# Encoder block on one core: f32 products and turns of an attention item side by side, queries normed inside the softmax, weight remainders and LN0 rows on VectorE

## The chip, the cores and the metric

The kernel runs on one core of a Trainium2 chip. Its time is device time in microseconds (us), from the start of the program on the core to its end; the times of the kernel before are those of three runs. The engines are named as the profile names them: PE is TensorE's matrix multiply (PEld its weight loads), DVE is VectorE, ACT is ScalarE, POOL is GpSimd, SP the engine that issues the DMAs.

## The reference, cut to what matters

One encoder layer for 512 tokens of width 1024, in float32: LayerNorm, a mixer of two attention branches, LayerNorm, an expert layer with 16 experts, LayerNorm.

```python
h = layer_norm(x, ln0_g, ln0_b)
proj = h @ w_in                                   # 1024 -> 5120, split into the parts below
qa, ka, va, qb, kb, vb, ga, gb = split(proj)      # 512, 128, 128, 768, 768, 768, 1024, 1024
# branch A: 8 query heads, 2 key heads, 64 wide
qa = rms_norm(qa, qn_g);  ka = rms_norm(ka, kn_g) # over the 64 of a head: y * rsqrt(mean(y*y) + eps) * gain
qa = rotary(qa, row, column); ka = rotary(ka, row, column)
ya = softmax(qa @ ka.T / 8) @ va @ w_branch_a
# branch B: 12 heads, three windows (128, 512, 2048) with strides 1, 4 and 16
qb = partial_rotary(qb); kb = partial_rotary(kb)
yb = combine(dilated_attention(qb, kb, vb)) @ w_branch_b
mix = (sigmoid(ga + b) * ya + sigmoid(gb + b) * yb) @ w_out
h = layer_norm(alpha * h + mix)
h = layer_norm(alpha * h + expert_choice_swiglu(h))   # each expert takes 64 tokens
```

## The kernel before

**Precision.** A matrix product of the mixer is three passes of the type fp32r: a value is split into a high part (`A.copy` into an fp32r tile) and the remainder (value minus high part), and `mm3` (lines 241 to 244) multiplies high by high, low by high and high by low. A call of `mm3` on 128x512 is a *unit*. Products of the attention on probabilities and the turns (transposes by a product with the identity) are plain f32.

**Weights.** `w_in` and the branch weights come in 46 tiles of 128x1024. `split(i)` (L211) lets ACT write the high part and POOL the remainder (L221); `split_to` keeps the splits two to three tiles ahead of the units that use them. A tile is used by eight units.

**Order.** The schedule is written by hand. Chunk 0 (the queries of branch A) is multiplied first. The other chunks of `w_in` stand as units in a queue (`gemm_units`, L402), with other work hooked in behind the n-th unit of a chunk: the norm and rotary of chunk 0 (`chain0a` to `chain0d`, and the turns `t_q`) run inside the units of chunk 1, those of keys in chunk 2 (`chain1a`, `chain1b`, `t_k`), the rotary of branch B (`rope_b` by `chain2`, `chain_b`) and its turns (`t_k0`, `t_b`) in chunks 3 to 5. `fill(ns)` takes units off the queue for so many ns, 650 each.

**Branch A** (from L756) has 16 items (a pair of heads and a block of 128 queries). Step n of its loop turns the probabilities of item n-1 (`a_trans`, two heads), computes the scores of item n (`a_scores`, fp32r), their softmax (`a_soft`: DVE finds the maximum, ACT takes exp, `a_norm`: DVE divides by the sum), and multiplies the turned probabilities of item n-1 with the values (`a_pv`). Six units are spread over it in four places. **Branch B** (from L842) does the same with 8 items and seven units in four places; its scores are f32.

[...]

**After the mixer** come the output product, LN1, the router with a top-64 search on DVE (TensorE multiplies idle products meanwhile, `keep_clock`), and 16 experts, whose 403 MB of weights stream through a ring of buffers; a buffer is loaded again when an expert has used it. The ring's first loads start as the mixer's buffers come free.

Of the kernel before, what the change touches and what calls it, by code (L numbers as in the profile page):

```python
# [47 lines left out]
def encoder_block(ctx, tc, x, ln0_g, ln0_b, w_in, b_gate, qn_g, kn_g, w_branch_a, w_branch_b,  # L48
# [53 lines left out]
    bPT = [misc[:, u0 + (4 + i) * 512:u0 + (5 + i) * 512] for i in range(2)]  # L102
# [107 lines left out]
    def split(i):  # L210
# [166 lines left out]

    def fill_until(name):
# [16 lines left out]
    def gemm_units(c, perm, evac, later=()):  # L395
# [4 lines left out]
        for kk in range(4):  # L400
            for m in range(NT):
                for j in range(2):  # L402
# [18 lines left out]
                    if k == KT - 1:  # L421
                        queue.append((0.0, lambda m=m: evac(m)))
# [56 lines left out]
    def chain0d(m):
        q4 = qhl[m % 2].rearrange("p (h v d) -> p h v d", h=8, v=2)  # L480
        t = heads(atmp[2 + m % 2])
        V.tensor_tensor(t, t, heads(atmp[m % 2]), OP.add)
        A.copy(q4[:, :, 0, :], t)
        V.tensor_tensor(q4[:, :, 1, :], t, q4[:, :, 0, :].bitcast(F32), OP.subtract)
# [41 lines left out]
    def chain1b():  # L526
        x4 = xall[:, :, 0:128].rearrange("p i (h d) -> p i h d", h=2)
        V.tensor_tensor(x4, x4, ssk.unsqueeze(3).to_broadcast([P, NT, 2, 64]), OP.mult)
        G.tensor_tensor(kt[0].rearrange("p i (h d) -> p i h d", h=2), x4,
                        ra[:, :, 128:192].unsqueeze(2).to_broadcast([P, NT, 2, 64]), OP.mult)  # L530
        for h in range(2):
            x5 = xall[:, :, h * 64:(h + 1) * 64].rearrange("p i (a b d) -> p i a b d", a=2, b=2)
            t5 = kt[1][:, :, h * 64:(h + 1) * 64].rearrange("p i (a b d) -> p i a b d", a=2, b=2)
            s5 = ra[:, :, 192:256].rearrange("p i (a b d) -> p i a b d", a=2, b=2)
            for b in range(2):
                V.tensor_tensor(t5[:, :, :, b, :], x5[:, :, :, 1 - b, :], s5[:, :, :, b, :], OP.mult)
# [91 lines left out]
    for m in range(NT):  # L628
        evac(0)(m)
# [1028 lines left out]
```

## Time and profile before

| | us |
|---|---|
| median of three runs (lowest to highest) | 1401.22 (1400.83 to 1401.72) |
| the profiled execution: device time | 1400.32 |
| its span, first to last instruction | 1398.2 |
| busy: PE, DVE, ACT, POOL | 1293.7, 431.3, 267.1, 155.2 |
[...]
| read from HBM, over the span | 437 MB, 314 GB/s |

Busy time is a sum over the span; where the span goes is read from the waits of PE stage by stage and from the chain of work that ended last. Matmuls overlap in the profile: one of 128x512 is shown as 0.39 to 0.40 us and the next starts 0.23 us after it, so the distance of two starts is its cost.

### The profile page before, as it was taken

The page shows a single profiled execution, that of the slowest core. Times are in us where ns is not written, and L with a number is a line of the kernel's source. Part 1 is how long each engine was busy: PE and PEld are TensorE (multiplying, and loading weights), DVE is VectorE, ACT ScalarE, POOL GpSimd, SP SyncE. Part 2 cuts the span into 40 slices and gives each one's busy share as a digit, 9 for nine tenths or more (in the row PEclk, how much of TensorE's full clock was granted, in tenths as well). Part 3 has the DMA queues.
Part 4 walks back from the last instruction along what each step waited for, and adds up shares of the span by engine and source line. Part 5 has one row for each costly group of instructions (what it writes and reads, how often), then busy time and mean ns, then how long its engine had stood idle before and what let it go on. Part 6 is the DMA issues. An engine that isn't in the chain of part 4 may idle for free.

```text
span 1398.2 us, 15300 instructions
## 1 busy us (share of the span) xinstructions
PE 1293.7 (93%) x6393; PEld 656.8 (47%) x6393; DVE 431.3 (31%) x805; ACT 267.1 (19%) x561; POOL 155.2 (11%) x75
## 2 busy tenths in 40 slices
PE   7899899999999899999999889879979988997994
PEld 6688798777787334333333223323322332332343
DVE  7755664556465213030021011102002011210206
ACT  4343344553234010010000000100001000010101
POOL 2544242224420000000000000000000000000001
PEclk9999999999999999999999999999999999999997
DMA  7111111114468789999999999999999999999995
GB/s 262 56 60 46 46 47 59 46 61 149 126 246 337 289 364 429 427 428 427 427 427 427 429 427 427 428 427 427 428 428 428 427 428 427 427 428 427 428 376 182
DMA packets 61323, 440.05 MB, mean 315 GB/s; under 512 B 7659, under 2 KB 23323, under 8 KB 36935
## 3 DMA queue, kind: packets, MB, share of 16 engines
q1 hardware_dynamic: 61255, 439.08, 76.6%
q8 instruction: 50, 0.82, 0.2%
q14 instruction: 18, 0.15, 0.0%
HBM read 436.96 MB, written 2.10 MB: 314 GB/s over the span
## 4 chain that ended last, share of the span: by engine, by line
PE 66%; DMA 25%; DVE 7%; ACT 1%; issue 0%; SPq 0%; DVEq 0%; ACTq 0%
DMA ring<-in_w_up_e_dram 20%; PE ps_o L1427 14%; PE ps_pj L1390 14%; PE ps_pj L242 7%; PE ps_pj L243 6%; PE ps_pj L244 6%; DMA ring<-in_w_down_e_dram 4%; PE ps_x L1440 4%; PE ps_x L1338 4%; PE ps_o L744 1%; PE ps_x L730 1%; PE ps_pj L1492 1%; PE ps_x L1354 1%; PE ps_x L1410 1%; DVE misc L476 1%; PE ps_x L821 0%
## 5 line engine op out<-in xcount | busy, mean ns | idle before, releaser
L1390 PE MATMUL ps_pj<-ring,misc 128*64 128x512 f32 x2032 | 449.9, 595 | 55.2 <-DMA ring<-in_w_up_e_dram 30.1
L1390 PEld LDWEIGHTS ps_pj<-ring,misc 128*64 128x64 f32 x2032 | 144.5, 137 | 351.4 <-issue 294.1
L1427 PE MATMUL ps_o<-ring,misc 128*64 128x512 f32 x928 | 218.5, 602 | 4.2 <-DVE misc L440 2.1
L1403 DVE SCALAR_TENSOR_TENSOR misc<-misc,gate,ps_pj 128x512 f32<-128x512 f32 x32 | 23.8, 747 | 445.8 <-PE ps_pj L1390 367.3
L1427 PEld LDWEIGHTS ps_o<-ring,misc 128*64 128x64 f32 x928 | 58.8, 136 | 136.1 <-issue 124.0
L221 POOL TENSOR_TENSOR whl<-misc,whl 128x1024 fp32r<-128x1024 f32 x38 | 92.6, 2443 | 210.0 <-ACT whl L216 189.6
L1551 POOL TENSOR_TENSOR merged<-merged,misc 128x512 f32<-128x512 f32 x2 | 3.0, 1486 | 939.3 <-ACT merged L1548 939.3
L242 PE MATMUL ps_pj<-whl,hT 128*128 128x512 f32 x192 | 90.5, 471 | 0.2 <-ACT hT L333 0.2
L1402 ACT ACTIVATE misc<-ps_pj 128x512 f32<-128x512 f32 x32 | 19.0, 597 | 364.9 <-PE ps_pj L1390 364.9
L243 PE MATMUL ps_pj<-whl,hT 128*128 128x512 f32 x192 | 78.5, 409 | 1.7 <-DVE hT L336 1.7
L244 PE MATMUL ps_pj<-whl,hT 128*128 128x512 f32 x192 | 78.0, 406 | 0.0
L1442 DVE TENSOR_TENSOR merged<-merged,ps_x 128x512 f32<-128x512 f32 x56 | 38.5, 687 | 102.9 <-PE ps_x L1440 102.9
L1359 ACT ACTIVATE misc<-ps_x,ln_bcol,ln_gcol 128x64 f32<-128x64 f32 x64 | 25.8, 403 | 210.1 <-DVE misc L1361 210.1
L1440 PE MATMUL ps_x<-misc,cst 128*128 128x512 f32 x112 | 63.0, 645 | 0.0
L1338 PE MATMUL ps_x<-hbuf,misc 128*64 128x512 f32 x256 | 59.5, 608 | 1.2 <-DVE misc L1325 1.2
L242 PE MATMUL ps_pj<-hT,whl 128*128 128x512 f32 x128 | 53.5, 418 | 0.9 <-DVE misc L688 0.9
L1361 DVE TENSOR_SCALAR misc<-ps_x,ln_gcol,ln_bcol 128x64 f32<-128x64 f32 x64 | 22.0, 344 | 104.5 <-PE ps_x L1354 81.8
L243 PEld LDWEIGHTS ps_pj<-whl,hT 128*128 128x128 f32 x192 | 50.2, 261 | 6.1 <-DVE hT L336 2.4
L242 PEld LDWEIGHTS ps_pj<-whl,hT 128*128 128x128 f32 x192 | 48.8, 254 | 7.3 <-issue 2.1
L244 PEld LDWEIGHTS ps_pj<-whl,hT 128*128 128x128 f32 x192 | 49.0, 255 | 4.5
L244 PE MATMUL ps_pj<-hT,whl 128*128 128x512 f32 x128 | 50.1, 392 | 0.0
L243 PE MATMUL ps_pj<-hT,whl 128*128 128x512 f32 x128 | 50.0, 391 | 0.0
(320 smaller groups left out, 1359.0 us busy)
## 6 DMA issues: line engine op xcount, KB each, us to landing
ring<-in_w_gate_e_dram SPq DMA_DIRECT2D x63, 2048.0 KB, 30.6
ring<-in_w_up_e_dram SPq DMA_DIRECT2D x62, 2048.0 KB, 27.0
ring<-in_w_down_e_dram SPq DMA_DIRECT2D x57, 2048.0 KB, 31.2
misc<-in_w_in_dram SPq DMA_DIRECT2D x22, 512.0 KB, 3.6
ring<-in_w_down_e_dram SPq DMA_DIRECT2D x12, 512.0 KB, 8.5
misc<-in_w_in_dram SPq DMA_DIRECT2D x20, 256.0 KB, 3.0
misc<-in_w_out_dram SPq DMA_DIRECT2D x8, 512.0 KB, 4.6
b_qk<-in_w_in_dram SPq DMA_DIRECT2D x6, 512.0 KB, 7.0
```

The lines of the kernel that those rows point to most:

```text
L221: G.tensor_tensor(lo, r, hi.bitcast(F32), OP.subtract)
L242: T.matmul(out_, sh, mh, start=start, stop=False)
L243: T.matmul(out_, sl, mh, start=False, stop=False)
L244: T.matmul(out_, sh, ml, start=False, stop=stop)
L1338: T.matmul(pg[64 * g:64 * g + 64, :], oneh[:, m, s * CAP:(s + 1) * CAP], zk[:, :, 4 * g:4 * g + 4], start=m == 0, stop=m == NT - 1)
L1359: A.activation(xeT[e % 2][:, k, :], src, AF.Identity, bias=bcol[:, k:k + 1], scale=gcol[:, k:k + 1])
L1361: V.tensor_scalar(xeT[e % 2][:, k, :], src, gcol[:, k:k + 1], bcol[:, k:k + 1], op0=OP.mult, op1=OP.add)
L1390: T.matmul(gu[which][t // 2][(t % 2) * 64:(t % 2) * 64 + 64, :], xe[:, k, :], w[:, kk % 2, :, 4 * t:4 * t + 4], start=k == 0, stop=k == KT ...
L1403: V.scalar_tensor_tensor(hh[t], sg[t], gate[e], gu[1][t], op0=OP.mult, op1=OP.mult)
L1427: T.matmul(py[n * 64:n * 64 + 64, :], hTe[:, j, :], w[:, n * 512:(n + 1) * 512], start=i == 0, stop=i == 15)
L1440: T.matmul(po, scat[:, m, :], ye[:, n * 512:(n + 1) * 512], start=True, stop=True)
L1442: V.tensor_tensor(a, a, po, OP.add)
```

## The change

- **Order on PE.** In branch A the two turns of item n-1, one turn for branch B (held back in the list `side` by `turn` and given out one per item, or all at once by `flush`) and the probability product of item n-2 stand in one group, straight in front of the scores; then come three units, the division, three units. In branch B the turns, the product of item n-2 and the scores stand together, then seven units. `bPT` gets two more buffers in `gb`.
- **Queries.** The queries aren't normed before the scores. The squares are summed aside, and the factor goes into the exp's scale and the maximum's factor (`qsc`). The rotary works on whole rows: ACT writes a copy with halves swapped (`q_copies`), DVE multiplies twice and adds (`q_turn`). The keys are multiplied by their factor after the rotary, and their swap is on ACT too.
- **POOL's work to DVE.** From tile 4 on the weight remainder is DVE's, and the LN0 gain and bias (two operations of 128x1024 per block on POOL) become 16 of 128x512 on DVE, two in each of the first 8 items.
- **Evictions.** In branch A's loop 7 of 8 evictions by `copy_any` go to ACT, in place of every second one, and branch A's turns are evicted by it too. The first three evictions of chunk 0 and the table product `ra` move ahead.
- **Router.** `keep_clock` runs 36 products in place of 30 during the search and 5 more ahead of the gather.

```diff
-    bPT = [misc[:, u0 + (4 + i) * 512:u0 + (5 + i) * 512] for i in range(2)]
+    bPT = [misc[...] for i in range(2)] + [gb[:, (1 + i) * 512:(2 + i) * 512] for i in range(2)]
...
-            G.tensor_tensor(lo, r, hi.bitcast(F32), OP.subtract)
+            (G if i < 4 else V).tensor_tensor(lo, r, hi.bitcast(F32), OP.subtract)
...
-    def ln0_gain(i):
-        G.tensor_tensor(hbuf[:, i, :], hbuf[:, i, :], gb[:, 0:1024], OP.mult)
-        G.tensor_tensor(hbuf[:, i, :], hbuf[:, i, :], gb[:, 1024:2048], OP.add)
+    def ln0_gain(n):
+        c = slice(n % 2 * 512, n % 2 * 512 + 512)
+        t = hbuf[:, n // 2, c]
+        V.tensor_tensor(t, t, gb[:, 0:1024][:, c], OP.mult)
+        V.tensor_tensor(t, t, gb[:, 1024:2048][:, c], OP.add)
...
+    def turn(fn):
+        return lambda: fn() if side[0] is None else side[0].append(fn)
+    def flush():
+        while side[0]:
+            side[0].pop(0)()
...
+    def q_copies(m):
+        A.copy(atmp[m].rearrange("p (h b d) -> p h b d", b=2, d=16), swapped(xtmp[m]))
+        A.activation(sq[m], xtmp[m], AF.Square)
+    def q_turn(m):
+        V.tensor_tensor(heads(xtmp[m]), heads(xtmp[m]), ra[:, m, 0:64]..., OP.mult)
+        V.tensor_tensor(heads(atmp[m]), heads(atmp[m]), ra[:, m, 64:128]..., OP.mult)
+        V.tensor_tensor(xtmp[m], xtmp[m], atmp[m], OP.add)
+    def q_split(m):
+        A.copy(q4[:, :, 0, :], t)
+        V.tensor_tensor(q4[:, :, 1, :], t, q4[:, :, 0, :].bitcast(F32), OP.subtract)
+    def q_sums(m):
+        V.tensor_reduce(ssq[:, m, :], heads(sq[m]), axis=AX.X, op=OP.add)
+    def q_scale():
+        rms_scale(ss)
+        rsqrt(ss, NT * 8, "q")
+        for v in range(2):
+            V.tensor_scalar(qsc[:, v], ssq, (SCALE, -SCALE)[v], None, op0=OP.mult)
...
     gemm_units(1, False, evac(1), [
-        (2, lambda: (chain0a(2), chain0a(3), chain0b())), (3, lambda: (chain0c(0), chain0c(1), chain0d(0))),
-        (8, ...), (12, ...), (16, lambda: t_q(0)), (17, ...), (20, lambda: t_q(1)), (21, ...), (26, lambda: t_q(2)), (30, lambda: t_q(3))])
+        (1, lambda: (q_copies(1), q_split(0), q_turn(1))), (3, lambda: (q_copies(2), q_split(1), q_turn(2))),
+        (7, lambda: q_copies(3)), (9, lambda: t_q(0)), (10, lambda: (q_split(2), q_turn(3))), (14, lambda: t_q(1)),
+        (15, lambda: (q_split(3), q_sums(0), q_sums(1))), (17, lambda: (q_sums(2), q_sums(3), q_scale())),
+        (21, lambda: t_q(2)), (24, lambda: t_q(3))])
...
     for n in range(len(items) + 1):
         if n >= 1:
-            a_trans(prev, 0)
-            fill(UNIT)
-            a_trans(prev, 1)
-            fill(UNIT)
+            for s in range(2):
+                a_trans((n - 1) % 2, s)
+            if side[0]:
+                side[0].pop(0)()
+        if n >= 2:
+            a_pv(*items[n - 2], n % 2)
         if n < len(items):
             st = a_scores(*items[n])
-            sm = a_soft(st, n % 2)
+            sm = a_soft(*items[n], st, n % 2)
...
-        fill(2 * UNIT)
+        if n < 8:
+            ln0_gain(n)
+        fill(3 * UNIT)
         if n < len(items):
             a_norm(sm, n % 2)
-        if n >= 1:
-            a_pv(*items[n - 1], prev)
-        fill(2 * UNIT)
+            fill(3 * UNIT)
...
-    keep_clock(30)
+    keep_clock(36)
...
+    keep_clock(5)
```

**PE in branch A**, from the turns of one item on. Before (L730 the turns, L242 to L244 a unit, L707 and L708 the scores; the product L744 follows two units later):

```order
L730 MATMUL ps_x<-cst,merged 128x128 x4
L242 MATMUL ps_pj<-whl_70,hT_67 128x512
L243 MATMUL ps_pj<-whl_70,hT_68 128x512
L244 MATMUL ps_pj<-whl_70,hT_67 128x512
L730 MATMUL ps_x<-cst,merged 128x128 x4
L242 MATMUL ps_pj<-whl_70,hT_67 128x512
L243 MATMUL ps_pj<-whl_70,hT_68 128x512
L244 MATMUL ps_pj<-whl_70,hT_67 128x512
L707 MATMUL ps_x<-a_qk 128x512
L708 MATMUL ps_x<-a_qk 128x512
```

Now, in the same place (L748 the turns, L581 a turn for branch B, L759 the product of the item before, L724 and L725 the scores):

```order
L748 MATMUL ps_x<-cst,merged 128x128 x8
L581 MATMUL ps_x<-cst,misc 128x128 x2
L759 MATMUL ps_o<-merged,misc 64x128 x8
L724 MATMUL ps_x<-a_qk 128x512
L725 MATMUL ps_x<-a_qk 128x512
L724 MATMUL ps_x<-a_qk 128x512
L725 MATMUL ps_x<-a_qk 128x512
L242 MATMUL ps_pj<-whl_69,hT_67 128x512
L243 MATMUL ps_pj<-whl_69,hT_68 128x512
L244 MATMUL ps_pj<-whl_69,hT_67 128x512
```

The units that stood between the f32 groups now stand behind the scores, and f32 and fp32r change places once per item.

**DVE in the twelfth item** (n = 11), where chunk 5 begins. Before (L715 and L716 the maximum, L722 and L725 the division, L500 to L504 the rotary):

```order
L715 TENSOR_REDUCE asm<-ps_x 128x1
L716 TENSOR_SCALAR asm<-asm 128x1
L715 TENSOR_REDUCE asm<-ps_x 128x1
L716 TENSOR_SCALAR asm<-asm 128x1
L722 RECIPROCAL asm<-asm 128x2
L725 TENSOR_SCALAR merged<-merged,asm 128x512 x2
L500 TENSOR_TENSOR misc<-misc,cst 128x512
L502 TENSOR_TENSOR misc<-misc,cst 128x32x8 x2
L504 TENSOR_TENSOR misc<-misc 128x32x16
```

Now (L732 and L734 the maximum, L221 the weight remainder, L517 to L521 the rotary, L740 and L743 the division):

```order
L732 TENSOR_REDUCE asm<-ps_x 128x1
L734 TENSOR_SCALAR asm<-asm,qsc 128x1
L732 TENSOR_REDUCE asm<-ps_x 128x1
L734 TENSOR_SCALAR asm<-asm,qsc 128x1
L221 TENSOR_TENSOR whl_70<-misc,whl_70 128x1024
L517 TENSOR_TENSOR misc<-misc,cst 128x512
L519 TENSOR_TENSOR misc<-misc,cst 128x32x8 x2
L521 TENSOR_TENSOR misc<-misc 128x32x16
L740 RECIPROCAL asm<-asm 128x2
L743 TENSOR_SCALAR merged<-merged,asm 128x512 x2
```

A remainder and a rotary have come in between the maximum and the division.

**ACT in chunk 1**, around the query norm. Before (L460 the squares, L143 and L144 the root, L483 the high part of the queries, L438 a turn's eviction):

```order
L460 ACTIVATE misc<-misc 128x512 x4
L143 ACTIVATE q_y<-ssq 128x32
L144 ACTIVATE q_y<-q_y 128x32
L483 CAST a_qk<-misc 128x8x64 x2
L216 CAST whl_70<-b_qk 128x1024
L438 CAST a_qk<-ps_x 128x4x128
```

Now (L452 a turn's eviction, L490 the high part of the queries):

```order
L452 CAST a_qk<-ps_x 128x4x128
L490 CAST a_qk<-misc 128x8x64
L216 CAST whl_69<-b_qk 128x1024
L143 ACTIVATE q_y<-ssq 128x32
L144 ACTIVATE q_y<-q_y 128x32
L452 CAST a_qk<-ps_x 128x4x128 x2
```

The root stood ahead of all turns and now stands between the evictions of the second turn and of the third and fourth.

## Rows read from the trace of the kernel before

**Rows 1.** Windows: PE, PEld, DVE, ACT, POOL busy (count), PE clock, DMA share, GB/s.

```profile
41.00:75.40 34.40, 28.29 (x130) 22.93 (x129) 27.87 (x35) 12.29 (x22) 18.40 (x9) 0.90 0.11 31
...
100.50:237.00 136.50, 130.10 (x774) 116.12 (x774) 78.87 (x158) 54.03 (x111) 48.58 (x20) 0.96 0.16 47
```

**Rows 2.** The chain that ended last, in the expert stage: start us, us, what.

```profile
674.65 26.15 DMA ring<-in_w_up_e_dram
```

**Rows 3.** Waits of PE, 28 to 465 us: total us, times, longest.

```profile
PE ps_x L491 <- DVE a_qk L484: 6.1, 2, 3.3
PE ps_x L730 <- DVE merged L725: 4.7, 1, 4.7
PE ps_o L744 <- DVE merged L734: 1.6, 1, 1.6
...
PE ps_pj L242 <- DVE misc L688: 0.9, 1, 0.9
```

**Rows 4.** Windows behind the third wait and around the L688 wait (columns of Rows 1).

```profile
110.00:113.00 3.00, 3.00 (x11) 2.35 (x10) 1.07 (x4) 0.83 (x3) 0.07 (x1) 0.50 0.00 0
...
371.00:376.00 5.00, 4.06 (x18) 3.05 (x17) 2.36 (x3) 1.95 (x2) 2.91 (x2) 1.00 0.46 164
```

**Rows 5.** Timeline, DVE and POOL in chunk 1: start us, us, engine, line, operation.

```profile
63.56 2.54 POOL L221 TENSOR_TENSOR whl<-b_qk,whl 128x1024 fp32r<-128x1024 f32 x1
...
64.41 2.25 DVE L482 TENSOR_TENSOR misc<-misc 128x512 f32<-128x512 f32 x1
```

**Rows 6.** Timeline, one item of branch A: scores, softmax, DVE and ACT between.

```profile
201.72 0.40 PE L242 MATMUL ps_pj<-whl,hT 128*128 128x512 f32 x1
...
202.15 0.68 DVE L715 TENSOR_REDUCE asm<-ps_x 128x1 f32<-128x512 f32 x1
...
202.43 0.40 PE L242 MATMUL ps_pj<-whl,hT 128*128 128x512 f32 x1
...
204.85 0.88 DVE L725 TENSOR_SCALAR merged<-merged,asm 128x512 f32<-128x512 f32 x2
...
204.98 1.07 ACT L216 CAST whl<-misc 128x1024 fp32r<-128x1024 f32 x1
```

**Rows 7.** Timeline, the same item: PE behind the product, then two groups of turns.

```profile
204.70 0.40 PE L243 MATMUL ps_pj<-whl,hT 128*128 128x512 f32 x1
...
205.87 0.60 PE L730 MATMUL ps_x<-cst,merged 128*128 128x128 f32 x4
...
206.31 0.60 PE L572 MATMUL ps_x<-cst,misc 128*128 128x128 f32 x4
...
207.10 0.40 PE L243 MATMUL ps_pj<-whl,hT 128*128 128x512 f32 x1
```

**Rows 8.** Timeline: single operations of DVE and ACT with nothing beside them on POOL.

```profile
196.22 0.57 ACT L438 COPY misc<-ps_pj 128x512 f32<-128x512 f32 x1
...
197.35 0.68 DVE L500 TENSOR_TENSOR misc<-misc,cst 128x512 f32<-128x512 f32 x1
...
388.33 1.23 DVE L934 TENSOR_TENSOR whl<-merged,whl 128x1024 fp32r<-128x1024 f32 x1 [6.78 <-ACT whl L933]
```

**Rows 9.** Timeline, DVE in the item in which chunk 4 begins.

```profile
150.04 5.08 DVE L502 TENSOR_TENSOR misc<-misc,cst 128x256 f32<-128x256 f32 x2
...
155.77 0.16 DVE L722 RECIPROCAL asm<-asm 128x2 f32<-128x2 f32 x1
```

**Rows 10.** Timeline, branch B: scores, the last sum of exp, a later table load.

```profile
270.12 1.71 PE L792 MATMUL ps_x<-b_qk 64*128 64x128 f32 x16
...
276.04 0.19 ACT L815 ACTIVATION_READ_ACCUMULATOR misc<-misc,bng 128x1 f32 x1
...
283.42 1.28 ACT L815 ACT_TABLE_LOAD   x1 [1.14 <-DVE bng L813]
```

**Rows 11.** The chain (start us, us, what): the router's gather and a later one.

```profile
460.79 5.38 PE ps_x L1338 x16
...
596.62 3.43 PE ps_x L1338 x16
```

More of the change, by code (lines that the diff above doesn't have):

```diff
@@ L101, in encoder_block @@
     bP = [misc[:, u0 + i * 512:u0 + (i + 1) * 512] for i in range(4)]
-    bPT = [misc[:, u0 + (4 + i) * 512:u0 + (5 + i) * 512] for i in range(2)]
+    bPT = [misc[:, u0 + (4 + i) * 512:u0 + (5 + i) * 512] for i in range(2)] + [gb[:, (1 + i) * 512:(2 + i) * 512] for i in range(2)]
     atmp = [misc[:, 4096 + i * 512:4096 + (i + 1) * 512] for i in range(4)]
@@ L421, in gemm_units @@
                     if k == KT - 1:
+                        if m == 0:
+                            queue.append((0.0, flush))
                         queue.append((0.0, lambda m=m: evac(m)))
@@ L526, in chain1b, with half @@
     def chain1b():
[L527 to L536, printed above, removed]
+        x3 = xall[:, :, 0:128]
+        def half(t, b):
+            return t.rearrange("p i (h b d) -> p i h b d", b=2, d=16)[:, :, :, b, :]
+        for b in range(2):
+            A.copy(half(kt[1], b), half(x3, 1 - b))
+        for t, src, c in ((kt[0], x3, 128), (kt[1], kt[1], 192)):
+            for h in range(2):
+                hs = slice(64 * h, 64 * h + 64)
+                V.tensor_tensor(t[:, :, hs], src[:, :, hs], ra[:, :, c:c + 64], OP.mult)
         V.tensor_tensor(kt[1], kt[1], kt[0], OP.add)
+        k4 = kt[1].rearrange("p i (h d) -> p i h d", h=2)
+        V.tensor_tensor(k4, k4, ssk.unsqueeze(3).to_broadcast([P, NT, 2, 64]), OP.mult)
         t = kt[1].rearrange("p i (h d) -> p i h d", h=2)
@@ L649, in gate_bias @@
         V.tensor_copy(bg, pt[:, 0:16])
-    gemm_units(5, True, evac5, sorted(after(chain_b, lambda m: t_b(2, m)) + [(24, gate_bias)], key=lambda t: t[0]))
+    gemm_units(5, True, evac5, after(chain_b, lambda m: t_b(2, m)) + [(24, gate_bias)])
     def evac_gate(c):
@@ L730, in a_trans @@
             T.transpose(pt[:, kt * P:(kt + 1) * P], aP[2 * par + s][:, kt * P:(kt + 1) * P], ident)
[L731 to L734 removed]
+        copy_any(aPT[2 * par + s], pt)
     ob = {}
@@ L843, in encoder_block @@
     items += [(g, p, 0) for g in (1, 2) for p in range(2)]
-    for n in range(len(items) + 1):
-        if n >= 1:
-            b_trans(n - 1, 0)
-            fill(2 * UNIT)
-            b_trans(n - 1, 1)
-            fill(1 * UNIT)
+    for n in range(len(items) + 2):
         if n < len(items):
             fill_until("chain2" if items[n][0] == 0 else "chunk5")
+            flush()
+        if 1 <= n <= len(items):
+            for s in range(2):
+                b_trans(n - 1, s)
+        if n >= 2:
+            g, p, ii = items[n - 2]
+            b_pv(g, p, ii, n - 2, g > 0 or ii == 1)
+        if n < len(items):
             st = b_scores(*items[n])
             b_soft(*items[n], st, n)
-        fill(2 * UNIT)
-        if n >= 1:
-            g, p, ii = items[n - 1]
-            b_pv(g, p, ii, n - 1, g > 0 or ii == 1)
-        fill(2 * UNIT)
+        fill((7 if n < len(items) else 1) * UNIT)
+    side[0] = None
     def nat(ap, g):
```

79 lines of the change are left out of this document (32 added, 47 removed).

## Prediction

> **What bounds the kernel now.** I read the windows by stage first, then the chain of waits, then PE's own waits, then the timeline of the stages that the change touches. In the expert stage PE waits for weights: one step of the chain is a wait of 26.15 us for a ring load [rows 2]. But that stream starts when the mixer's buffers come free and runs on from the first expert's use of them, so whatever the mixer and the router save or lose moves the end by the same amount. Up to there PE is the bound; what can be won is its waits, its clock and its own work. The waits between 28 and 465 us are few: 6.1 us for two query turns, 4.7 and 1.6 us in branch A, 0.9 us later [rows 3]. All have DVE as releaser. [...] Chunk 1 has a mean clock of 0.90 over 34.4 us: 0.10 x 34.4 = 3.4 us lost [rows 1], some 1.7 us behind each of its waits. Branch A has 0.96 over 136.5 us: 5.5 us, of which PE was idle in part; I count 3.9.
>
> **The change part by part.** The sum is made against the profiled execution, 1400.3 us, 0.9 under the median.
>
> *Queries in chunk 1.* Before, the turns wait for the norm, which stands first. Now the norm isn't in their way. From the end of chunk 0 (41 us) DVE does, ahead of the first turn, an eviction, three operations of a rotary, a remainder and a query remainder: 5 x 0.68 + 1.23 = 4.6 us [rows 8], while PE has nine units of 0.71, the distance of two in rows 6: 6.4 us. So the first two waits, 6.1 us, and their 3.4 us of clock go: -9.5. What comes late next: the second half of the fourth turn needs the PSUM buffer of the third turn's first half (three buffers go round), whose eviction now stands on ACT behind the root of the queries, and that waits for DVE's sums. DVE's work up to there: 4 rotaries of 3, 4 query remainders, an eviction, 2 turn copies, 4 sums, all at 0.68, and 3 remainders at 1.23: 23 x 0.68 + 3.7 = 19.3, with 1.5 us of waiting for ACT's high parts 20.8; then the copy, 0.57, behind two small operations of ACT, some 0.5: 62.9 us. PE is there after 24 units and three and a half turns of 8 x 0.11 [rows 7]: 41 + 17.0 + 3.1 = 61.1. A wait of 1.8 (0 to 3, as ACT's part is rough), with 1.7 us of clock behind it, as behind the 1.6 us one. Chunk 1: -9.5 + 3.5 = -6.0, between -9.5 and -3.
>
> *Groups on PE.* From rows 7: eight turns and one product take 207.10 - 205.87 = 1.23 us, where 8 x 0.11 (four turns take 0.44) and 0.235 would do: each passage through f32 costs 0.12. From 202.43 [rows 6] to 204.70 lie four fp32r products and the sixteen of L744: 2.27 less 0.94 and 8 x 0.11 leaves 0.45 for that group. Two of three passages of an item go; a product into half of the columns may keep its own price between turns and scores. So 2 x 0.12 per item at least, 0.12 + 0.45 at most: 16 items give 3.8 to 9; I take 4.5, near the lower end, since the column change stays. Branch B, 8 items, two of four passages: 2 to 5, I take 2.5.
>
> *DVE in branch A* is where the change can lose. DVE's slack: the first maximum starts at 202.15, the first half of the division ends 3.14 us later [rows 6]; the first head's scores are done two products (0.47) before the scores end, so DVE can start some 0.26 before that end. So the turns are ready 2.95 us behind the scores, PE comes after six units of 0.71 = 4.23: 1.3 us to spare. Into the queue between maximum and division come: (a) LN0, two operations, 1.4 us in 8 items; exp takes most of that time, so 0.6, hidden. (b) In 4 of 16 items (n = 3, 7, 11, 15) a remainder. It waits for its high part, which ACT writes after both exps (1.07), then takes 1.23: 2.4 us late, 1.1 us of wait, three times. (c) n = 11: an eviction on ACT (0.57) and a rotary (2 x 0.68 + 2 x 0.42 = 2.2) as well: 4.0. (d) n = 6: the rotary, behind LN0: 1.7. (e) n = 1: a remainder, a rotary and a copy of the values at the end of item 0: 1.3. Together 10.4 us, against 6.3 before [rows 3]: +4.1. Behind n = 6 and 11, and with even chance n = 1, the clock: 4.3 against 3.9. POOL's absence helps: 512 elements took 2.25 us beside POOL's remainder [rows 5], 0.68 alone [rows 8], and two of 256 took 5.08 [rows 9]; the prices above are those without POOL. Branch A: 4.1 + 0.4 - 4.5 = 0.0, between -10 (no wait of (b) to (e)) and +6.
>
> The order of DVE's queue carries 10 us of this. In rows 9 the reciprocal at 155.77 stands behind 5.08 us of rotary, though its sums were long there: nothing passes. [...] If the division could pass, the sum would be 10 us lower.
>
> *Branch B.* The turns come seven units (5.0 us) behind the scores; the exps end 276.2 - 271.8 = 4.4 us behind them [rows 10], so 0.6 is spare. Where the gates of chunk 6 switch ACT's table, there and back, two loads of 1.28 [rows 10] delay an item's exps. Some 1.2 of their 2.6 us lies in the item's spare time and its successor's: +1.4, less 0.3 that the old order lost there: +1.1 (0 to 3). With the groups -1.4, between -5 and +1.
>
> *Router.* The gather (L1338) took 5.38 us at the lower clock, 3.43 in a later one [rows 11]. PE idled between search and gather; 36 and 5 products fill that. -1.9 if the clock then holds; if not, or if the last products delay the search's result, up to +0.5.
>
> *At no cost*: evictions moved to ACT (54 of 136 us busy in branch A [rows 1]), LN0 in 16 pieces beyond (a), the two buffers, the bias load moved. The key swap leaves DVE with as much as before.
>
> Sum: -6.0 + 0.0 - 1.4 - 1.9 = -9.3, on the profiled execution 1391.0; on the median 1401.2 - 9.3 = 1391.9.
>
> **The rivals.** *DVE keeps ahead in branch A*: the high parts are written earlier, or a division is less late than I count, so that (b) to (e) don't wait. For it: DVE is busy 78.9 of 136.5 us [rows 1], and part of that is time beside POOL. Against it: the order of the queue. Gain: 10.4 + 4.3 = 14.7; 1377, or halfway 1385. *DVE becomes the bound of branch A*, slower than before: the place is the division of every item. DVE loses POOL's 48.6 us of help there [rows 1], which cost it about half: 12 remainders of 1.23 and 16 LN0 operations of 0.68 are 26 us. If ACT, with seven of eight evictions, comes 1 us later with its exps, the 1.3 us are gone with (a), and all 16 items wait; at 0.9 us each and the clock behind half of them: 14 + 8 x 1.0 = 22 more, 1414; it makes the kernel slower than before by over 0.2% from 12 us more on, 1404. *The queries still wait* in chunk 1: the second and third turn are held by ACT's copies (1.2 us per block ahead of each rotary), so that only half of 9.5 goes: 1397 to 1401. *Grouping gives nothing*, since the passage costs by the column change alone: 4.5 + 2.5 back: 1399.
>
> **How the numbers follow.** The forecast 0.55 (1386 to 1398), DVE keeps ahead 0.20, queries still wait or grouping gives nothing 0.15, DVE the bound 0.10. The likeliest gives 1391.9. The range takes in chunk 1's and branch A's bounds and most of the rivals: 1380 to 1402; left out are the far end of the first rival and that of the slower one. About 0.2% (2.8 us) is what a measurement of this kernel tells from no change. Faster: nearly all of 0.55, 0.20 and a third of 0.15: 0.78. Same: 0.12. Slower: 0.10.
>
> **What the profile would show.** Right: no wait of PE for the first query turns; one of 1 to 3 us at the fourth, released by ACT; waits of the turns (L748) for DVE's division (L743) at some five items, the longest near the start of chunk 5; DVE's 128x1024 remainder at 1.2 us; the gather at 3.4 us; the first ring load some 8 us earlier, and the expert stage shifted as a whole. Wrong: waits of L748 in every item, or in none; clock losses in branch A above 6 us; an end that doesn't move with the gather.

## The result, and the profile after

The changed kernel takes **1392.25 us** (median of 4 runs, 1389.03 to 1393.52) against 1401.03 before (4 runs, 1400.27 to 1401.72): a ratio of **0.9943**, 95% interval 0.993 to 0.9956, faster by 8.8 us. The forecast was 1391.9 with a range of 1380 to 1402. The sum came out; several of its terms did not, and that is what the experiments are about.

The profiled execution took 1393.52 us (span 1391.5, mean granted clock 0.988; before, 0.986). I cut it where the 33rd, 65th, 97th, 193rd and 321st unit (L242) of the mixer start on PE: chunk 1, chunk 2, chunks 3 to 5 (branch A), then B with the combine stage, then the rest. Windows of the kernel after, columns as in [rows 1]:

```profile
10.70:41.80 31.10, 28.01 (x125) 22.33 (x126) 25.69 (x48) 16.80 (x36) 6.43 (x3) 0.95 0.65 230
41.80:67.70 25.90, 24.88 (x129) 20.66 (x128) 21.77 (x36) 13.51 (x23) 0.00 (x0) 1.00 0.12 40
67.70:92.85 25.15, 25.15 (x126) 20.72 (x124) 17.67 (x37) 10.54 (x21) 0.00 (x0) 1.00 0.28 84
92.85:225.45 132.60, 125.29 (x782) 113.67 (x782) 77.81 (x162) 66.97 (x136) 0.00 (x0) 0.97 0.16 49
225.45:357.04 131.59, 126.47 (x685) 100.12 (x684) 80.10 (x121) 58.02 (x139) 0.20 (x1) 0.96 0.28 89
357.04:1391.50 1034.46, 952.99 (x4549) 377.73 (x4547) 214.67 (x420) 111.94 (x231) 15.20 (x11) 0.99 0.94 395
```

Three stages of the kernel before that [rows 1] doesn't hold, cut at the same units:

```profile
10.90:41.00 30.10, 28.07 (x125) 22.33 (x126) 21.04 (x44) 16.15 (x34) 9.55 (x5) 0.94 0.67 235
237.00:362.10 125.10, 124.50 (x691) 94.27 (x690) 71.07 (x105) 57.88 (x139) 39.29 (x16) 1.00 0.30 93
362.10:1398.20 1036.10, 951.87 (x4538) 376.31 (x4536) 212.75 (x416) 111.94 (x231) 25.76 (x16) 0.99 0.94 394
```

Chunk 1 went from 34.4 to 25.9 us, branch A from 136.5 to 132.6. B and the combine stage went the other way: 125.1 us at a clock of 1.00 became 131.6 at 0.96. The rest is 1.6 shorter; chunk 1 starts 0.8 later. The waits of PE from 28 to 465 us (as in [rows 3]) tell where the new losses lie:

```profile
PE ps_x L748 <- DVE merged L743: 6.7, 4, 3.5
PE ps_pj L242 <- DVE merged L679: 2.4, 1, 2.4
PE ps_x L815 <- ACT misc L452: 2.0, 1, 2.0
PE ps_x L508 <- ACT a_qk L452: 1.0, 1, 1.0
```

The two query waits of 6.1 us are gone; 1.0 at the fourth turn is new. L748, the turns of the probabilities in A, wait for the division in four items. Two waits have no counterpart before: 2.0 us in B and 2.4 in the combine stage. At three of these waits the granted clock falls to 0.50, as it does in [rows 4] behind the wait of 1.6 us, while it is 1.00 there around the wait of 0.9:

```profile
183.40:190.20 6.80, 5.24 (x28) 4.32 (x29) 2.63 (x7) 0.58 (x1) 0.00 (x0) 0.50 0.24 74
268.80:275.60 6.80, 6.59 (x19) 5.40 (x20) 5.22 (x9) 4.11 (x14) 0.00 (x0) 0.50 0.46 154
323.40:326.80 3.40, 3.40 (x9) 2.65 (x9) 1.18 (x2) 2.18 (x2) 0.00 (x0) 0.50 0.92 307
```

In the second of them products of 128x512 start 0.43 us apart (271.61, 272.04, 272.46), just behind it 0.23 (275.98, 276.21). I count half of PE's busy time in them as lost: 2.6 us in A, 5.0 in B and the combine stage. The longest wait of A (item 11, 3.5 us) in the timeline of ACT and DVE:

```profile
178.66 0.78 ACT L736 ACTIVATE merged<-ps_x,asm,qsc 128x512 f32<-128x512 f32 x1
...
179.43 0.58 ACT L452 COPY misc<-ps_pj 128x512 f32<-128x512 f32 x1
179.90 1.06 ACT L216 CAST whl<-misc 128x1024 fp32r<-128x1024 f32 x1
...
180.99 1.22 DVE L221 TENSOR_TENSOR whl<-misc,whl 128x1024 fp32r<-128x1024 f32 x1 [2.36 <-ACT whl L216]
182.13 0.68 DVE L517 TENSOR_TENSOR misc<-misc,cst 128x512 f32<-128x512 f32 x1
...
183.52 0.69 DVE L521 TENSOR_TENSOR misc<-misc 128x512 f32<-128x512 f32 x1
184.13 0.16 DVE L740 RECIPROCAL asm<-asm 128x2 f32<-128x2 f32 x1
```

The last exp is over by 179.5. DVE is idle for 2.36 us, since the remainder that stands next in its queue waits for the cast by which ACT writes the high part; then come the remainder and the rotary, and the reciprocal of the division starts at 184.13, 4.6 us after its input. In B it is ACT's queue: a table load, the sigmoid of the gate and two casts stand ahead of the copy that frees one of the three PSUM buffers of scores and turns (`ps_x`) for the second head's scores. Timeline of ACT and PE:

```profile
263.39 1.28 ACT L681 ACT_TABLE_LOAD   x1
264.69 1.91 ACT L681 ACTIVATE merged<-merged 128x2048 f32<-128x2048 f32 x1
266.50 1.98 ACT L216 CAST whl<-misc 128x1024 fp32r<-128x1024 f32 x2
268.39 0.57 ACT L452 COPY misc<-ps_x 128x512 f32<-128x512 f32 x1
...
269.01 2.07 PE L815 MATMUL ps_x<-b_qk 64*128 64x128 f32 x8 [2.04 <-ACT misc L452]
```

### The profile page after: what moved, and what is told of

The parts are those of the page before. It is cut to its first block, busy times and chain, and to the rows that moved or that the text cites. A ratio compares the mean times of both kernels' runs of the same rounds, so it can differ in the third digit from the quotient of the medians.

```text
span 1391.5 us, 15293 instructions
## 1 busy us (share of the span) xinstructions
PE 1287.9 (93%) x6404; PEld 659.1 (47%) x6404; DVE 443.5 (32%) x836; ACT 282.9 (20%) x592; POOL 24.9 (2%) x20
## 4 chain that ended last, share of the span: by engine, by line
PE 63%; DMA 25%; DVE 7%; ACT 3%; issue 1%; ACTq 0%; DVEq 0%
DMA ring<-in_w_up_e_dram 18%; PE ps_pj L1414 15%; PE ps_o L1451 14%; DMA ring<-in_w_down_e_dram 7%; PE ps_pj L242 6%; PE ps_pj L243 5%; PE ps_pj L244 5%; PE ps_x L1464 4%; PE ps_x L1362 3%; PE ps_o L759 1%; PE ps_x L748 1%; PE ps_pj L1516 1%; DVE whl L221 1%; PE ps_x L1378 1%; ACT whl L216 1%
## 5 line engine op out<-in xcount | busy, mean ns | idle before, releaser
L242 PE MATMUL ps_pj<-whl,hT 128*128 128x512 f32 x192 | 78.3, 408 | 0.5 <-ACT hT L335 0.5
L243 PE MATMUL ps_pj<-whl,hT 128*128 128x512 f32 x192 | 76.4, 398 | 1.5 <-DVE hT L338 1.5
L244 PE MATMUL ps_pj<-whl,hT 128*128 128x512 f32 x192 | 76.3, 398 | 0.0
L221 DVE TENSOR_TENSOR whl<-misc,whl 128x1024 fp32r<-128x1024 f32 x38 | 46.1, 1222 | 36.7 <-ACT whl L216 36.7
L242 PE MATMUL ps_pj<-hT,whl 128*128 128x512 f32 x128 | 51.9, 406 | 0.9 <-ACT misc L452 0.7
L243 PEld LDWEIGHTS ps_pj<-whl,hT 128*128 128x128 f32 x192 | 48.3, 252 | 5.7 <-DVE hT L338 2.2
L242 PEld LDWEIGHTS ps_pj<-whl,hT 128*128 128x128 f32 x192 | 48.2, 251 | 5.5 <-ACT hT L335 0.9
L244 PE MATMUL ps_pj<-hT,whl 128*128 128x512 f32 x128 | 49.9, 390 | 0.0
L244 PEld LDWEIGHTS ps_pj<-whl,hT 128*128 128x128 f32 x192 | 48.1, 250 | 3.9
L216 ACT CAST whl<-misc 128x1024 fp32r<-128x1024 f32 x38 | 39.4, 1044 | 21.7 <-DMA misc<-in_w_branch_b_dram 8.5
```

Of the source, the lines that this page charges most:

```text
L216: A.copy(hi, r)
L221: (G if i < 4 else V).tensor_tensor(lo, r, hi.bitcast(F32), OP.subtract)
L242: T.matmul(out_, sh, mh, start=start, stop=False)
L243: T.matmul(out_, sl, mh, start=False, stop=False)
L244: T.matmul(out_, sh, ml, start=False, stop=stop)
```

## The experiments

Ratios are to the kernel before, run beside each (medians 1398.5 to 1400.0). Stages are cut as above.

### The parts apart

**e1**, the query part alone: the rest of the diff is undone.

> The kernel before with the query part alone (products and turns of an item spread among the units again, weight remainders and LN0 rows on POOL, one keep_clock before the router's counts). Theory 'the query part pays, the rest nets out': in the trace of the changed kernel chunk 1 is 8.5 us shorter, branch A 3.9 shorter, B 2.9 and the combine 3.6 longer, the router 1.9 shorter, the start 0.8 longer; so the query part alone gives chunk 1 in 25.9 +- 1 us and a total of 1401 - 8.5 + 0.8 = 1393.3 (1391.5 to 1395). Rival 'the parts lean on each other' (the fourth query turn comes off well only because the remainders have left POOL, whose work held DVE back): chunk 1 28 to 31 us, a total of 1396 to 1399.

Measured: 1397.18 us, ratio 0.9985 (0.9976 to 0.9994). Chunk 1 took 28.7 us, not 25.9: the rival. PE waits 2.6 us for DVE from 44.9 on, and branch A, with its old order, took 140.1 (clock 0.95; waits of 4.7 and 3.8, each with the lower clock behind it), 3.6 more than before. So of the 5.7 us gained in chunk 1 the query part alone kept 1.8.

**e2**, the weight remainders and LN0 back on POOL:

```diff
-            (G if i < 4 else V).tensor_tensor(lo, r, hi.bitcast(F32), OP.subtract)
+            G.tensor_tensor(lo, r, hi.bitcast(F32), OP.subtract)
...
-        V.tensor_tensor(t, t, gb[:, 0:1024][:, c], OP.mult)
-        V.tensor_tensor(t, t, gb[:, 1024:2048][:, c], OP.add)
+        G.tensor_tensor(t, t, gb[:, 0:1024][:, c], OP.mult)
+        G.tensor_tensor(t, t, gb[:, 1024:2048][:, c], OP.add)
```

> The changed kernel with all weight remainders and the LN0 rows back on POOL. Theory 'DVE's queue makes the waits of branch A': the waits of the probability turns (L748, 6.7 us in all) and the half-clock stretch behind the longest fall to under 3 us, A is 4 to 7 us shorter, the total 1385 to 1389. Rival 'POOL was the dearer place' (while POOL works, DVE's own instructions beside it wait or stretch): the waits of A stay at 6 us or above, A is no shorter, the total 1392 to 1398. In the combine stage both remainders' theories say the same of the wait of 2.4 us at 319.87: if the queue of DVE makes it, it shrinks to under 1.

Measured: 1389.99 us, ratio 0.9926 (0.9913 to 0.994), not to be told from the changed kernel, but by another way. Chunk 1 is 2.8 us longer. The wait of 2.6 us is there again, and the timeline of the chunk's start shows where DVE loses the time (first the row of PE's wait, then POOL and DVE):

```profile
PE ps_pj L242 <- DVE misc L454: 2.6, 1, 2.6
...
37.69 5.01 POOL L221 TENSOR_TENSOR whl<-misc,whl 128x1024 fp32r<-128x1024 f32 x2 [17.29 <-ACT whl L216]
42.65 2.84 POOL L221 TENSOR_TENSOR whl<-b_qk,whl 128x1024 fp32r<-128x1024 f32 x1
...
40.54 2.71 DVE L483 TENSOR_TENSOR misc<-misc,b_qk 128x512 f32<-128x512 f32 x1 [2.47 <-ACT merged L479]
43.18 2.86 DVE L484 TENSOR_TENSOR misc<-misc,b_qk 128x512 f32<-128x512 f32 x1
```

The two products of the rotary end 0.55 us behind POOL's instructions (43.25 after 42.70, 46.04 after 45.49); in the kernel after, where POOL does nothing between 18.3 and 244 us, the same two take 0.69 and 0.68. So beside POOL's remainders they took 2.02 and 2.18 us more; what ties the two engines together, no run shows.

In branch A the waits of L748 did not fall: 6.9 us. The remainders had left DVE's queue, but at item 6 two rotary products of 256 took 2.94 us beside POOL (0.75 in the kernel after), and the division stood behind them as before:

```profile
139.09 2.94 DVE L519 TENSOR_TENSOR misc<-misc,cst 128x256 f32<-128x256 f32 x2
```

My expectation of under 3 was wrong; the waits are the rival's, but the total lies between the ranges of the two. Moving POOL's work to DVE, taken by itself, made no difference in the total that the runs can tell. B and the combine stage took 125.0 us at clock 1.00: there the wait of 2.0 us is gone, though ACT's queue reads the same. The second head's scores now wait for DVE's copy, not for ACT's, so they have another PSUM buffer: they are done by 269.8, while ACT's copy starts at 270.67. The wait in the combine stage stayed (2.2), so it isn't the remainder on DVE that makes it.

**e3**, products and turns spread among the units as before, the rest as changed.

> The changed kernel with the products and turns of an item of A and B spread among the units as before (remainders and LN0 rows still on VectorE, the query part and the router as changed). Theory 'grouping pays by the passages between f32 and fp32r work': the prediction's 4.5 us of A and 2.5 of B come back, and the total is 1392.3 + 7 = 1399 (1396 to 1402); branch A's waits for DVE are 10 us or more, since the turn of an item then follows its norm at the same distance. Rival 'the groups' gain is eaten by what they wait for': B loses its wait of 2.0 us at 266.7 with its half-clock stretch (3.4), so that B is shorter by 3 and A longer by 4: the total 1392 to 1394.

Measured: 1393.34 us, ratio 0.9957 (0.9944 to 0.9969): the rival's total, but not by its reason, as the wait in B was there (2.3). A took 135.0 us, 2.4 more, with 7.3 us of waits but no clock loss; B and the combine stage took 129.2, 2.4 less, with 1.5 us less of waits and 3.3 less of clock. Without waits and clock A takes 127.7 us here and 122.7 in the kernel after: PE's own work is shorter by 5.0 with the groups, and the clock of A and the waits and clock of B took that back. Whether it pays in the total needed a kernel without these waits (e12).

### The order of the queues

**e4**: in branch A the weight remainder and the rotary of branch B (the chain) that a `fill` issues come behind the item's division. `hold` puts them on a list, `release` issues them; the loop's part of the edit:

```diff
+        held[0] = []
         fill(3 * UNIT)
         if n < len(items):
             a_norm(sm, n % 2)
+        release()
+        if n < len(items):
             fill(3 * UNIT)
```

> The changed kernel; in branch A the remainder's subtract (with the load that reuses its buffer) and the rope chains that a fill issues ahead of an item's norm are issued right behind that norm. Nothing is taken away. Theory 'DVE works its queue in order, and the norm stands behind the remainder and the chain': the waits of L748 (6.7 us; 0.98 at items 3 and 7, 1.29 at item 6, 3.47 at item 11) go to under 1 us in all, the half-clock stretch 183 to 190 goes with them (3.4), and the total is 1382 to 1386. Rival 'the exps on ACT end last': the waits stay above 4 us with ACT as the releaser, the total 1390 to 1393. Rival 'a later remainder is the next thing that is late': new waits of the units for the remainder (L221 or L242 against DVE), the total 1388 to 1393.

Measured: **1381.61 us**, ratio 0.9872 (0.9858 to 0.9885), the first theory on every count and 0.4 below its range. No wait of L748 for DVE is left, branch A takes 122.6 us at clock 1.00, 10.0 less: 6.7 of waits and 2.6 of clock are most of it. The units did not miss the later remainders. Item 11 in its timeline (the sums come at 176.6, the remainder and the rotary now follow the division):

```profile
176.60 0.17 DVE L749 RECIPROCAL asm<-asm 128x2 f32<-128x2 f32 x1 [0.94 <-ACT merged L745]
176.81 0.88 DVE L752 TENSOR_SCALAR merged<-merged,asm 128x512 f32<-128x512 f32 x2
178.03 1.23 DVE L230 TENSOR_TENSOR whl<-misc,whl 128x1024 fp32r<-128x1024 f32 x1 [0.34 <-ACT whl L225]
```

**e5**: only the chains are held, the remainders not.

> As the run with the deferred queue (1381.6, ratio 0.9872), but only the three rope chains are issued behind the norm; the remainders' subtracts stand ahead of it again. Theory 'both stand in the norm's way': of the 6.7 us of waits of L748 the chain's share at item 11 (3.47, of which four chain instructions of 0.7 to 0.8 are the larger part) falls to about 1, items 3, 6 and 7 keep 0.98, 1.29 and 0.98, the half-clock stretch at 183 goes: waits of 3 to 4.5 us, total 1384 to 1387. Rival 'the chain is everything': waits under 1, total 1380 to 1383. Rival 'the remainder is everything': waits of 5 or more, total 1389 to 1392.

Measured: 1385.34 us, ratio 0.9899 (0.9885 to 0.9914); waits of 0.98, 0.99 and 1.47 at items 3, 7 and 11, 3.4 us in all, no clock loss in A, which took 126.6. Both stand in the way, each with about half of the waits.

**e6**: as e4, and in B the whole split (cast, remainder, load) is held until the next item's turns are issued.

> As the run with the deferred queue; in branch B too a whole split (ACT's cast, DVE's subtract, the load behind them) that a fill issues is issued right behind the next item's turns. Theory 'what stands ahead of the copy in ACT's queue makes the wait': the wait of 2.0 us at L827 (257.6 in the run with the deferred queue) loses the two casts of 0.99 each and goes to about 0; its half-clock stretch (261.4 to 264.8, 1.7) goes: total 1381.6 - 3.7 = 1377.9 (1377 to 1380). Rival 'the table load and the sigmoid alone are long enough' (1.28 + 1.91 from 263.39 on in the changed kernel's trace, the turn at 266.4): a wait of 0.3 to 1 stays, with or without the stretch: 1379 to 1381. Rival 'the casts are missed elsewhere': the units behind wait for a late remainder by 1 us or more: 1381 to 1384.

Measured: 1382.58 us, ratio 0.9877 (0.9859 to 0.9894), no gain on e4. The wait at the copy is gone; a new one of 1.4 us stands at the next item's turns, for the exps, and behind it the clock is at 0.50 for 10.2 us. DVE's timeline says why the exps are late:

```profile
257.29 2.36 DVE L231 TENSOR_TENSOR whl<-misc,whl 128x1024 fp32r<-128x1024 f32 x2 [2.50 <-ACT whl L226]
259.57 0.68 DVE L846 SCALAR_TENSOR_TENSOR misc<-ps_x,cst 128x512 f32<-128x512 f32 x1
```

The remainders, held only until the turns, stood waiting for the casts ahead of the softmax's first operation (L846). A wait had been moved from one queue to the other; I had not listed DVE's side.

**e7**: as e4, with an exponential in place of the gate's sigmoid, so that ACT loads no second table in B (e4 has two loads of 1.28 us between 250 and 275, this run none; the kernel then computes another gate).

> As the run with the deferred queue, but the gate of the first half of branch A's output is an exponential instead of a sigmoid (that part of the computation is changed), so that ACT keeps its table there: the two table loads of 1.28 us in B (263.39 and 272.13 in the changed kernel's trace) are not needed. Theory 'the table load makes the wait in B': the wait of 2.0 us falls to about 0.7, and the half-clock stretch behind it goes: total 1381.6 - 1.3 - 1.7 = 1378.6 (1378 to 1380). Rival 'the wait counts little, the units catch up': total 1380.5 to 1382.5, wait 0.7 all the same. Rival 'the loads are hidden': the wait stays at 2.0.

Measured: 1378.36 us, ratio 0.9852 (0.9836 to 0.9868), 2.8 us (0.9872 - 0.9852) less than e4, though the two intervals overlap. The wait fell from 2.0 to 1.0, and no lower clock follows it. In e4 and here:

```profile
PE ps_x L827 <- ACT misc L461: 2.0, 1, 2.0
PE ps_x L827 <- ACT misc L461: 1.0, 1, 1.0
```

About half of the wait goes with the table load; e6 shows that all of it goes with the casts.

**e8**: as e6, the sigmoid held too, and the second half's gates taken out of PSUM by ACT instead of DVE.

> As the run in which B's splits are held, and two things more: the first gate's sigmoid (with its table load) too is issued behind the turns' copies, and the second half's gates are taken out of PSUM by four sigmoids on ACT with the bias inside, where four DVE copies (L679 of the changed kernel, 0.74 each) and one sigmoid of 1.91 stood. Theory 'each wait is what stands ahead in a queue': both waits of PE (2.0 in B, 2.4 in the combine stage) and the half-clock stretches behind them (1.7 each) go: 1381.6 - 2.0 - 2.4 - 3.4 = 1373.8 (1373 to 1377). Rival 'the queue of ACT takes the place of DVE's' (table load 1.28 and four sigmoids of 0.6 behind the cast of the combined output): the wait in the combine stage stays at 1.5 to 3, now for ACT: 1376 to 1379. Rival 'the sigmoid is late for the product behind it': the branch products' evictions wait, units wait for their banks: 1379 to 1383.

Measured: 1383.7 us, ratio 0.9888 (0.9874 to 0.9903), no better than e4. The wait in the combine stage is the first rival's, now for ACT; the total is above its range (1376 to 1379), and the wait at the turns that e6 had is here too, longer. The two waits:

```profile
PE ps_pj L252 <- ACT merged L687: 3.0, 1, 3.0
PE ps_x L859 <- ACT misc L853: 2.5, 1, 2.5
```

In the combine stage ACT's table load and sigmoids took the place of DVE's evictions: giving the evictions to another engine doesn't remove the wait (e11 changes their order instead).

**e9**: the changed kernel once more, beside the next two.

> The changed kernel once more, on the chip and beside the runs of the two versions sent with it, since its runs scattered by 4.5 us (1389.0 to 1393.5) and the kernel before by 1.5. Theory 'the half-clock stretches differ from run to run, the waits don't': a ratio to before of 0.993 to 0.995, waits of PE in branch A of 6.7 +- 0.3 and in B of 2.0 again, half-clock stretches partly at other places. Rival 'the first runs were lucky': ratio 0.996 or more.

Measured: 1390.62 us (1387.42 to 1392.67), ratio 0.9933 (0.992 to 0.9947). The waits in its trace are the same to 0.1 us (6.7, 2.4, 2.0, 1.0), with the lower clock at the same three; that it would fall partly at other places was wrong for this trace. Chunk 0 took 29.9 us, where the first profile's took 31.1.

**e10**: as e4, and in B each queue by itself: casts behind the turns' copies on ACT, remainders behind the softmax's operations on DVE.

> As the run with the deferred queue, and in B the casts behind the turns' copies on ACT, the remainders behind the softmax's vector work on DVE (in the run where both went right behind the turns, DVE's two remainders stood waiting for the casts ahead of the next item's vector work, and the wait of 2.0 for the copy became one of 1.4 for the exps). Theory 'each queue has its own urgent work, and the remainder must stand behind it': neither wait is there (under 0.4 in all from 250 to 280), no half-clock stretch from 255 to 280: a ratio of 0.9872 - 0.0026 = 0.9846 (0.983 to 0.986). Rival 'ACT is full there' (exps 3.2, table loads 2 x 1.28, sigmoid 1.91, casts 1.98, copies 1.2 in one item of some 9): a wait of 1 to 2 stays for the exps: 0.986 to 0.988.

Measured: 1377.05 us, ratio 0.984 (0.9827 to 0.9852). No wait from 250 to 280, B and the combine stage 125.0 us at clock 1.00. The wait of 2.4 in the combine stage is still there, in this execution without the lower clock that e4's had (1.7 us).

**e11**: as e10, and in the combine stage the gate evictions ahead of the last remainder and the split.

```diff
     def combine2(p):
         o_ = bP[1]
+        if p == 1:
+            held[0] = []
...
             fill(UNIT)
+        if p == 1:
+            fill(6 * UNIT)
+            release()
         A.copy(oB[:, 0, p, :], o_)
```

> As the run before it, and in the combine stage the gate evictions come ahead of the last remainder and of the split of the combined output on DVE. Theory 'DVE's order makes the wait of 2.4': the remainder (1.22) and the split (0.69, itself waiting 0.68 for ACT's cast) stood between the product's last sum and the first eviction, so the wait goes to 0 to 0.5, with its half-clock stretch (1.7): 0.0026 less than the run before it, 0.982 (0.9805 to 0.9835), 1373 to 1375 us. Rival 'the sum itself is late' (L941 at 308.25 waits for PE's spread of the weights): the wait stays at 1 or more: 0.983 to 0.985.

Measured: **1373.87 us** (4 runs, 1373.71 to 1374.01), ratio **0.9816** (0.9803 to 0.9828). This version beats both kernels: it takes 16.8 us less than the changed one run beside it (e9). The windows of its two stages:

```profile
92.10:214.60 122.50, 121.89 (x782) 111.84 (x781) 77.44 (x162) 66.96 (x136) 0.00 (x0) 1.00 0.18 53
214.60:338.10 123.50, 122.01 (x684) 95.97 (x683) 80.28 (x121) 58.18 (x139) 0.20 (x1) 1.00 0.30 94
```

DVE's timeline at the end of the combine stage. In the kernel after, the split of the combined output (L934), which waits for ACT's cast, stands between the last sum (L931) and the evictions (L679):

```profile
319.88 0.69 DVE L931 TENSOR_TENSOR misc<-misc 128x512 f32<-128x512 f32 x1
321.26 0.69 DVE L934 TENSOR_TENSOR a_qk<-misc,a_qk 128x512 fp32r<-128x512 f32 x1 [0.68 <-ACT a_qk L933]
321.87 2.72 DVE L679 TENSOR_SCALAR merged<-ps_pj,misc 128x512 f32<-128x512 f32 x4
```

In e11 the evictions (L693) start right behind the last sum (L956):

```profile
303.07 0.69 DVE L956 TENSOR_TENSOR misc<-misc 128x512 f32<-128x512 f32 x1
303.68 2.06 DVE L693 TENSOR_SCALAR merged<-ps_pj,misc 128x512 f32<-128x512 f32 x3
305.66 1.22 DVE L235 TENSOR_TENSOR whl<-misc,whl 128x1024 fp32r<-128x1024 f32 x1
```

**e12**: as e11, but in branch A products and turns are spread among the units as in the kernel before; branch B keeps its groups.

> The version with all three queues put right (ratio 0.9816, branch A from 92.1 to 214.6: 122.6 us), but in branch A an item's products and turns spread among the units as in the kernel before. With hardly a wait left in A, this prices the grouping itself. Theory of the prediction (fewer passages between f32 and fp32r work on PE, 4.5 us, bounds 3.8 and 9): A takes 126.4 to 131.6, the likeliest 127.1, without more waits; ratio 0.9816 + 0.0032 = 0.985 (0.984 to 0.988). Rival 'grouping pays by time for DVE, not by passages' (the turn now follows its norm after two units instead of three): waits of L748 of 3 us or more in all, and A less those waits within 2 us of 122.6. Rival 'grouping is worth nothing here': A 122 to 124, ratio 0.981 to 0.983.

Measured: 1382.07 us, ratio 0.9879 (0.9862 to 0.9895), by the ratios 8.8 us above e11 (7.5 between the two profiled executions). The window of its branch A, and the waits that were L748 (here L762):

```profile
92.00:220.60 128.60, 126.97 (x775) 113.66 (x775) 78.28 (x162) 67.32 (x136) 0.00 (x0) 1.00 0.17 50
```

```profile
PE ps_x L762 <- DVE merged L757: 1.6, 4, 0.6
```

A is 6.1 us longer than in e11, with 1.6 us of such waits against none, and though the eight score products of B at the end of e11's window stand behind it here. PE is busy for 5.1 us more (126.97 against 121.89): the grouping pays on PE itself. Whether it does so by the passages between f32 and fp32r or by the changes of columns, which became fewer with them, no run separates.

## Why the prediction was right, and where it was not

I split each stage into waits of PE (gaps over 0.15 us), the clock's loss (half of the time without waits at clock 0.50) and the rest:

| us | before: rest + waits + clock | after: rest + waits + clock | change | forecast |
|---|---|---|---|---|
| until chunk 1 | 41.0 | 41.8 | +0.8 | 0 |
| chunk 1 | 34.4 | 25.9 | -8.5 | -6.0 |
| branch A | 126.2 + 6.3 + 4.0 | 122.7 + 7.3 + 2.6 | -3.9 | 0.0 |
| B and combine | 124.8 + 0.2 + 0 | 121.5 + 5.1 + 5.0 | +6.5 | -1.4 |
| router and rest | 1036.1 | 1034.5 | -1.6 | -1.9 |
| span | 1398.2 | 1391.5 | -6.7 | -9.3 |

The median moved by 8.8; the profiled execution of the changed kernel is the slowest of its four.

*Queries in chunk 1*: the first waits went with their clock, as said (-9.5). The late thing at the fourth turn came too, for ACT's copy, but with 1.0 us (forecast 1.8, bounds 0 to 3) and without the 1.7 us of clock. That is the miss of 2.5. The forecast priced DVE without POOL beside it; e1 and e2 show that 2.8 us of the 8.5 hang on that.

*Groups on PE*: forecast 4.5 in A and 2.5 in B. The rest of A fell by 3.5, but A now holds 8 score products of B that stood behind it before (782 against 774, 1.1 us from start to start), so the groups gave 4.6 there and 3.3 - 1.1 = 2.2 in B. Against e3 and e12 they save 5.0 and 5.1 us in A, and those products come on top: some 6. So A's price lies between 4.6 and 6, in the bounds of 3.8 and 9 worked out from [rows 7], and the choice near the lower end was a little low. B's groups were not tested alone.

*DVE in branch A*: the mechanism was right, the size too large. Forecast were waits at n = 3, 7, 15 (1.1 each), 11 (4.0), 6 (1.7) and 1 (1.3); measured were 0.98, 0.98, none, 3.47, 1.29 and under 0.3. With the small waits of A that makes +1.0 where +4.1 was written; item 15 and item 1 are the misses. The clock behind them cost 2.6 instead of 4.3. The step on the queue's order was tested by e4, and the mechanism holds: with the order changed the waits go. That A then falls by 10.0, the figure of the step, is luck: the 10 were waits alone (10.4, with 4.3 of clock to come on top), and the 10.0 measured are 6.7 of waits, 2.6 of clock and 0.7 of other things. (Two small sums in that working are off, without effect: the terms add up to 10.3, and 3.14 less 0.26 is 2.88, not 2.95.)

*Branch B and the combine stage* are the step that failed. I charged the table loads with 1.1 us, as a delay of exps that PE meets seven units later. What ended the wait was not the exps but a copy, queued behind the table load, the sigmoid and the casts, that frees a PSUM buffer (2.0 us, shown by e7, e6 and e10 together). The combine stage I did not look at: its evictions stand behind the split of the combined output (2.4 us, shown by e11). And at both the clock fell, 5.0 us. The runs e1 to e3 tell which part of the change brought each wait. The one at the copy is there where the remainders and LN0 are on DVE (after, e3) and absent where they are on POOL (before, e1, e2). The one in the combine stage is there at 2.4 and 2.2 us where B's work is in groups (after, e2), at 1.0 in e3 and absent in e1 and before: with B spread, units fall at other places of the stage, and in the kernel before the first of the four gate evictions (L662) comes 5 us ahead of the last split (L911):

```profile
326.76 0.74 DVE L662 TENSOR_SCALAR merged<-ps_pj,misc 128x512 f32<-128x512 f32 x1
...
331.82 0.69 DVE L911 TENSOR_TENSOR a_qk<-misc,a_qk 128x512 fp32r<-128x512 f32 x1
```

So, as far as these five traces show, the groups in B, written as a gain of 2.5, brought 1.4 to 2.2 us of this wait with them. With a wait of 0.7 at the start of B, and 0.2 lost before, that is +9.9 where +1.1 stood. Excess in chunk 1 and A (2.5 + 3.9) and shortfall here (7.9) nearly cancel; that the sum came out is partly luck.

*Router*: right. The gather's group in the chain ([rows 11] has 5.38; the granted clock is 0.68 there, from 460.8 to 466.2, and 1.00 in the kernel after, from 455.0 to 458.6), and the chain's first ring load ([rows 2] has it at 674.65):

```profile
455.02 3.65 PE ps_x L1362 x16
...
667.16 25.91 DMA ring<-in_w_up_e_dram
```

e1, with the old filling products, has 5.38 again. The ring load came 7.5 us earlier and the end 6.7: the expert stage shifted as a whole but for 0.8, as the prediction's first step has it.

*The start* was not in the sum. In the first profile a DVE operation on one element a row (L137) took 2.31 us beside POOL's remainder, where it takes 0.16; in e9 the stage has its old length (29.9 us); in e4 the longest wait of ACT in this stage, for DVE, is 5.6 us as in the first profile, in e2 3.3. So the same kernel has it in one execution and not in another; whether the kernel before ever has it, its one trace doesn't show.

*The rivals*: "DVE keeps ahead" gave 1377 to 1385 for a branch A without waits; that is what e4 measured once the order was changed by hand (1381.6). "DVE becomes the bound" and "grouping gives nothing" are out by e4 and e12; DVE's busy time in A even fell a little (78.9 to 77.8 us), though it took over some 26 us of work, as its own operations no longer stretch beside POOL (two products of 256 take 0.75 and 0.76 us, in [rows 9] 5.08) and seven of eight evictions went to ACT. "The queries still wait" is out by the waits of the changed kernel: the two of 6.1 us are gone. What the evictions on ACT are worth alone was not tested.

## What to carry to other kernels

Work that is moved onto an engine was paid here not by that engine's load (DVE was busy 78 of 133 us) but by whoever waited for the instruction queued behind it. So issue such work right behind the instruction that another engine waits for, on every queue it touches, and look for the next urgent instruction on each (e6 forgot one). A stage that loses nothing before can lose after; read each stage up to the join, not only those that the change names. A sum that comes out right is no proof of its terms: compare stage by stage.

## What the runs showed of the hardware that I had not expected

The lower clock doesn't follow a wait's length strictly. In the traces of all kernels, the waits of PE in the mixer from 28 us on that lasted 2.8 to 4.7 us all have a stretch at 0.50 with them (ten waits); of those between 2.0 and 2.6 us, nine have one (the kernel after, e3, e4, e7, e8, e9) and seven have none (e1, e2, e3, e5 in B, e6, e10; e5's in the combine stage is left open), the same wait of 2.4 in the combine stage on both sides; and a shorter one of 1.4 us (e6) has one, as does the one of 1.6 in the kernel before. The stretches last 3.4 or 6.8 us, once 10.2 (e6), and I count half of that as lost. So one wait of 2 us costs 2 us in one place and, as I estimate from the kernel after, about 4 or 5 in another (2.4 + 1.7 in the combine stage, 2.0 + 3.3 in B), and this is part of the scatter of the runs: in e9 the mean clock of the whole execution is 0.988 and 0.989 in the two slowest (1392.7 and 1392.5 us) and 0.993 in the two fastest (1387.4 and 1388.0). The runs of e11, whose clock is 1.00 in branch A and in B and the combine stage, lie within 0.3 us; but e12's is 1.00 in the same stages too, and its runs scatter over 3.5. What decides it I did not test.
